# Convolution stage of a two-layer trunk: wider copies of y, statistics of the last chunk by token, another order around the norm, three tap groups on another engine

## The chip, the cores and the metric

The kernel runs on one core of a Trainium2 chip. The metric is the device time of one execution in microseconds. Three executions of the kernel before took 1098.86, 1101.70 and 1102.46 us. The core has five engines with a queue each: TensorE (PE) for matrix products, VectorE (DVE), ScalarE (ACT) and GpSimd (POOL) for elementwise work, and SyncE (SP), whose queue here issues nearly all DMAs. Each queue is worked off in order; an instruction that waits holds up all that is queued behind it.

## The reference

Two layers run over 256 latent and 256 context tokens of width 1024. The first layer's mixer is a convolution module, and the change lies in it:

```
y = h @ w1 + b1;  a, gt = split(y);  y = a * sigmoid(gt)
y = depthwise_conv(y, dw, width 31, padding 15) + dw_b
y = silu(layer_norm(y, norm_g));  return y @ w2
```

The layer norm is over the 1024 channels of a token: it takes off the mean and scales by the inverse deviation. Each sub-layer has a shift, a scale and a gate, which come from SiLU(c) @ ada_w + ada_b; a SwiGLU FFN follows, then the second layer (retention, FFN). All is float32; products with weights are made in three passes of a split into a high and a low part.

## The kernel before, in words

Channels lie on partitions, in eight chunks of 128; the 512 columns are the 256 latent and the 256 context tokens. A loop over eight steps (L633) makes the chunks one after the other. In step s TensorE makes the two halves of W1's product for chunk s (`pair_half`, 24 matmuls each, L573), and GLU gives y of chunk s: by ScalarE and GpSimd, for chunk 7 by VectorE (`glu`, L470). The 31 taps of a chunk's depthwise convolution are divided: the first 4 x GROUPS[ch] go to TensorE, the last POOL[ch] to ScalarE and GpSimd, those between to VectorE (`dwconv_dve`, L530), one instruction each over 128x512. `GROUPS` (L49) has 4 for every chunk, so a chunk has 16 taps on TensorE and 9 on VectorE, 10 for chunk 7. In step s VectorE works on chunk s-1: five taps, then the low part of the next W1 block (`w1_lo`), then `total(s-2)`, the sum of the three partial results, then the other taps.

For TensorE's taps, y goes through DRAM. `bounce_out` (L483) writes it with one DMA. `bounce_in` (L489) loads a table `dg` and then reads y back with four DMAs, shifted by 0 to 3 columns, so that each partition of `z4` holds one of 32 channels of four quarters at one of four shifts. One run of such a read is 569 numbers, 2,276 bytes. `dwconv_pe` (L500) then makes four taps with each group: four fp32 matmuls onto 32 partitions each, which the profile counts as eight. Every DMA of this part is issued by SP, in program order.

`square` and `stats` (L562, L566) sum a chunk's values and squares over its channels into four rows of a PSUM tile `pst`. After chunk 7, ScalarE copies `pst` to `srow`; TensorE turns it by token into `ptk` (L752) and spreads the mean over all partitions into `pmd` (L755); ScalarE copies that to `mb`, and GpSimd takes it off all eight chunks (L771). VectorE makes the inverse deviation in 14 small instructions (L773 to L796), TensorE spreads it (`token_row`, L776), and a loop over chunks (L815) multiplies (`z_norm`), takes the Silu on ScalarE and splits z in two parts. Then come the products with W2 in two halves of columns, n = 0 and 1, each of 96 matmuls (8 k, 4 token tiles, 3 passes).

Around this, 20 blocks of ada_w are worked in as filler. A block has four parts: `begin` (16 matmuls of sums on TensorE), `evict` (ScalarE), `cols` (TensorE, 4 short matmuls) and `finish` (ScalarE). Blocks 8 to 15 run between step 7 and z, 16 and 17 in the z loop, 18 and 19 in the first half of W2. Their rows are loaded into whatever buffer is free: two large tiles that the W1 activations leave (`fills`), the two `z4` buffers, small tiles for the blocks in `ADA_K4`, or the three buffers for weight rows (`raw`). `gate_to_rows` and `gate_bc` (L280, L293) send the gate through DRAM so that the residual after W2 can use it.

Instructions marked with `pin` keep the order in which the program gives them; the others, among them most of W2's products, are put in place by the planner that builds the queues. The order in this stage is thus mostly written out by hand.

Of the kernel before, what the change touches and what calls it, by code (L numbers as in the profile page):

```python
# [47 lines left out]
K_PAIRS = 2  # L48
GROUPS = [4, 4, 4, 4, 4, 4, 4, 4]  # L49
POOL = [6, 6, 6, 6, 6, 6, 6, 5]  # L50
# [11 lines left out]
PACC = 2  # L62
ADA_AUX = (16, 17, 18, 19)
ADA_K4 = (8, 9, 18)
T2 = 5
# [16 lines left out]
def trunk_kernel(ctx: ExitStack, tc, x_in, ctx_in, cond, small, consts, rope, dist, ada, adas, adat,  # L82
# [483 lines left out]
    def stats(ch):  # L566
        for i, src in enumerate((yc[:, ch, :], sqs.pop(ch))):
            q = 2 * (ch % 2) + i
            pin(nc.tensor.matmul(pst[32 * q:32 * q + 32, :], mean32, src, start=(ch < 2), stop=(ch >= KC - 2)))

# [138 lines left out]
    dve_taps(d, 0, cut)  # L709
    total(c)  # L710
    dve_taps(d, cut, TAPS)

    fills = [pA.tile([P, 4096], F32, tag=tag, name=f"raw_fill_{tag}") for tag in ("ah", "al")]
    pin(nc.gpsimd.memset(fills[0][:, 0:1], 0.0))
    for i in range(12, 16):
        t = fills[(i - 12) // 2][:, 2048 * (i % 2):2048 * (i % 2) + 2048]
# [3 lines left out]
    for i in (16, 17):  # L720
        t = cv.tile([P, 4, 2 * YW], F32, tag="z4", name=f"raw_ada{i}", bufs=Z4).rearrange("p q t -> p (q t)")[:, 0:2048]
        pin(nc.sync.dma_start(t, ada[ADA_PE.index(i)]))
        ada_raws[i] = halves(t)
    cols(8)
# [9 lines left out]
    evict(10)  # L734
    stats(c)
    cols(10)
    finish(10)
    begin(11)
    cbs[d] = dwconv_pe(d, zs4.pop(d))
    evict(11)  # L740
    cols(11)
    total(d)
    finish(11)
    square(d)
    stats(KC - 1)
    begin(12)
    srow = t2("srow")
    pin(nc.scalar.activation(srow, pst, AF.Copy))
    evict(12)
    ptk = aux("stats_t")  # L750
    for t in range(4):
        pin(nc.tensor.matmul(ptk[:, 2 * t:2 * t + 2], srow[:, P * t:P * t + P], sel2, start=True, stop=True))  # L752
    pmd = aux("mean_bc")
    for q in range(4):
        pin(nc.tensor.matmul(pmd[32 * q:32 * q + 32, :], sel2[:, 0:1].to_broadcast([P, 32]), srow, start=True, stop=True))  # L755
    mb = cv.tile([P, 512], F32, tag="sq", name="mb", bufs=2)
    begin(13)
    cols(12)
    pin(nc.scalar.activation(mb, pmd, AF.Copy))
    evict(13)  # L760
    finish(12)
    cols(13)
    finish(13)
    gate_to_rows(0, 0, pin)
    gates = [gate_bc(0, 0, 0, pin), gate_bc(0, 0, 1, pin)]
    ada_raws[18] = ada_load(18, pin)
    ada_raws[19] = ada_load(19, pin)
    begin(14)
    evict(14)
    for ch in range(KC):  # L770
        pin(nc.gpsimd.tensor_tensor(yc[:, ch, :], yc[:, ch, :], mb, op=ALU.subtract))  # L771
    st = cv.tile([P, 4, 2], F32, name="st")
    nc.vector.tensor_copy(st.rearrange("p t i -> p (t i)"), ptk[:, 0:8])  # L773
    md, vv = st[:, :, 0], st[:, :, 1]

# [21 lines left out]
    prs = token_row(rn, "rstd_bc")  # L797
    cols(14)
    finish(14)
    begin(15)  # L800
    evict(15)
    cols(15)
    finish(15)

# [10 lines left out]
    for ch in range(KC):  # L815
# [5 lines left out]
        if ch == W2_AT:  # L821
            split_w2(0, 1, None, pin)
        if ch in (2, 4):
            begin(15 + ch // 2)
            evict(15 + ch // 2)
        if ch in (3, 5):
            cols(15 + ch // 2)
            finish(15 + ch // 2)
# [34 lines left out]
    for n in range(2):  # L863
# [7 lines left out]
        for t, k in order:  # L871
# [3 lines left out]
            if k == KC - 1:  # L875
                residual(t, n, pw[t], gates[t // 2], last)
            if not n and t == 3 and k in (3, 5):
                begin(18 + k // 5)
                evict(18 + k // 5)
            if not n and t == 3 and k in (4, 6):  # L880
                cols(18 + k // 6)
                finish(18 + k // 6)
            if n and (t, k) == (1, KC - 1):
# [567 lines left out]
```

## Time and profile before

| what | value |
|---|---|
| profiled execution | 1103.33 us, of which 1101.2 us are the span from first to last instruction |
| median of the runs | 1101.70 us (1098.86 to 1102.46) |
| PE / DVE / ACT / POOL busy, of the span | 97% / 64% / 38% / 15% |
| mean granted TensorE clock | 0.991 of full speed |
| chain that ended last | PE 86%, DVE 6%, DMA 4%, ACT 3%, issue 1% |
| DMA | 190 MB, mean 173 GB/s |
| z from yd, 32 DMAs of 284.5 KB | median 4.9 us from issue to landing |

Times in the views count from the start of the span. In a timeline a row has its start, its duration, the engine, the line, the operation, the result and the sources, and in brackets the idle time of the engine ahead of it with what ended it. In a table of windows each engine has its busy time and its count of instructions; the last three numbers are the granted clock (1.00 is full), the mean busy share of the DMA engines and the rate in GB/s. A matmul row lasts longer than its turn, since matmuls overlap; the chain shows the turns.

### The profile page before, as it was taken

Reading aid. Unit: us, or ns where it says so; the run is one execution under the profiler, and the core shown is the slowest. Engines: PE = TensorE matmul, PEld = TensorE weight load, DVE = VectorE, ACT = ScalarE, POOL = GpSimd, SP = SyncE. Lnnn points to the kernel's source line nnn. Section 1 sums busy time; section 2 is a strip of 40 time slices with the busy share of each in tenths; the row PEclk is TensorE's granted clock in tenths of the full one; section 3 lists DMA queues with packets and bytes.
Section 4 is the critical chain, followed back from the end, with each engine's and each line's share of the span. In section 5 each row is a group of like instructions: output and inputs, shape, how many; then the busy total and the mean of one; then the engine's idle time right before and its main releaser. Section 6 shows DMA issues by size and latency. Waiting matters only on the chain.

```text
span 1101.2 us, 13492 instructions
## 1 busy us (share of the span) xinstructions
PE 1069.0 (97%) x5302; PEld 845.0 (77%) x5302; DVE 700.6 (64%) x1147; ACT 417.5 (38%) x607; POOL 161.6 (15%) x119
## 2 busy tenths in 40 slices
PE   6989998999999999999999999999999989999998
PEld 2766654789888888888888788888888868888886
DVE  3988873757999877545644796366364555555445
ACT  4474463343222122212232564234333454444442
POOL 0077853030000000000000330000000461000000
PEclk8999998999999999999999999999999999999999
DMA  9469778732566576533313342334333344455551
GB/s 372 181 179 264 223 195 348 265 115 99 191 248 249 201 296 234 186 114 116 115 59 132 135 143 106 115 134 155 113 115 115 115 152 155 172 190 191 190 182 49
DMA packets 35185, 190.29 MB, mean 173 GB/s; under 512 B 3953, under 2 KB 4401, under 8 KB 16177
## 3 DMA queue, kind: packets, MB, share of 16 engines
q1 hardware_dynamic: 34688, 187.87, 49.0%
q10 hardware_dynamic: 434, 1.55, 0.4%
q8 instruction: 42, 0.69, 0.3%
q14 instruction: 21, 0.17, 0.0%
HBM read 185.99 MB, written 3.42 MB: 172 GB/s over the span
## 4 chain that ended last, share of the span: by engine, by line
PE 86%; DVE 6%; DMA 4%; ACT 3%; issue 1%; SPq 0%; POOL 0%; ACTq 0%; DVEq 0%
PE u L202 4%; PE fa L201 4%; PE u L200 4%; PE u L201 4%; PE fa L202 4%; PE fb L201 4%; PE fb L202 4%; PE fa L200 4%; PE fb L200 4%; PE v L201 3%; PE v L202 3%; PE v L200 3%; PE dn L201 3%; PE dn L202 3%; PE dn L200 3%; PE cv L507 2%
## 5 line engine op out<-in xcount | busy, mean ns | idle before, releaser
L171 DVE TENSOR_TENSOR wl_gu<-raw_gu,wh_gu 128x1024 fp32r<-128x1024 f32 x76 | 92.2, 1223 | 82.6 <-ACT wh_gu L163 81.7
L163 ACT ACTIVATE wh_gu<-raw_gu 128x1024 fp32r<-128x1024 f32 x84 | 88.0, 1058 | 139.6 <-PE fb L201 52.6
L851 DVE SCALAR_TENSOR_TENSOR junk<-raw_adat,crow 128x1024 f32<-128x1024 f32 x80 | 97.5, 1219 | 0.9
L171 DVE TENSOR_TENSOR wl_dn<-raw_dn,wh_dn 128x1024 fp32r<-128x1024 f32 x38 | 46.5, 1224 | 45.3 <-ACT wh_dn L163 45.0
L200 PE MATMUL fa<-ah_h0f,wh_gu 128*128 128x512 f32 (+1 forms) x192 | 72.0, 376 | 1.0 <-DVE ah_h0f L324 1.0
L201 PE MATMUL fa<-al_h0f,wh_gu 128*128 128x512 f32 (+1 forms) x192 | 72.3, 376 | 0.1
L200 PE MATMUL fb<-ah_h0f,wh_gu 128*128 128x512 f32 (+1 forms) x192 | 72.1, 376 | 0.0
L202 PE MATMUL fa<-ah_h0f,wl_gu 128*128 128x512 f32 (+1 forms) x192 | 72.0, 375 | 0.0
L202 PE MATMUL fb<-ah_h0f,wl_gu 128*128 128x512 f32 (+1 forms) x192 | 72.0, 375 | 0.0
L201 PE MATMUL fb<-al_h0f,wh_gu 128*128 128x512 f32 (+1 forms) x192 | 72.0, 375 | 0.0
L163 ACT ACTIVATE wh_dn<-raw_dn 128x1024 fp32r<-128x1024 f32 x38 | 40.3, 1060 | 80.1 <-PE dn L202 35.5
L200 PE MATMUL u<-wh_gu,ah_h1f 128*128 128x512 f32 x160 | 63.5, 397 | 0.0
L171 POOL TENSOR_TENSOR wl_qk<-raw_qk,wh_qk 128x1024 fp32r<-128x1024 f32 x4 | 9.6, 2401 | 362.8 <-DVE res L355 350.3
L202 PE MATMUL u<-wh_gu,al_h1f 128*128 128x512 f32 x160 | 62.8, 393 | 0.0
L201 PE MATMUL u<-wl_gu,ah_h1f 128*128 128x512 f32 x160 | 62.2, 390 | 0.0
L523 POOL TENSOR_TENSOR pacc<-pacc,pr 128x512 f32<-128x512 f32 x39 | 58.8, 1508 | 17.8 <-ACT pr L522 15.5
L540 DVE SCALAR_TENSOR_TENSOR lacc<-y,sm,lacc 128x512 f32<-128x512 f32 x65 | 49.1, 755 | 2.1
L201 PE MATMUL v<-wl_v,ah_h 128*128 128x512 f32 x128 | 50.4, 393 | 0.0
L202 PE MATMUL v<-wh_v,al_h 128*128 128x512 f32 x128 | 50.1, 391 | 0.0
L200 PE MATMUL dn<-wh_dn,ah_hid 128*128 128x512 f32 x128 | 49.9, 390 | 0.0
L201 PE MATMUL dn<-wl_dn,ah_hid 128*128 128x512 f32 x128 | 49.8, 389 | 0.0
L202 PE MATMUL dn<-wh_dn,al_hid 128*128 128x512 f32 x128 | 49.8, 389 | 0.0
(308 smaller groups left out, 2669.5 us busy)
## 6 DMA issues: line engine op xcount, KB each, us to landing
raw_gu<-in_gu_dram SPq DMA_DIRECT2D x44, 1024.0 KB, 4.8
raw_adat<-in_adat_dram SPq DMA_DIRECT2D x28, 1024.0 KB, 4.9
raw_dn<-in_dn_dram SPq DMA_DIRECT2D x19, 1024.0 KB, 4.8
raw_ada<-in_ada_dram SPq DMA_DIRECT2D x10, 1024.0 KB, 10.8
z<-yd SPq DMA_DIRECT2D x32, 284.5 KB, 4.9
raw_qk<-in_wqk_dram SPq DMA_DIRECT2D x8, 1024.0 KB, 4.7
raw_v<-in_wv_dram SPq DMA_DIRECT2D x8, 1024.0 KB, 4.8
raw_g<-in_wg_dram SPq DMA_DIRECT2D x8, 1024.0 KB, 4.8
```

The lines of the kernel that those rows point to most:

```text
L163: also(nc.scalar.activation(hi[:, :m], raw[:, c:c + m], AF.Copy))
L171: also((eng or nc.vector).tensor_tensor(lo[:, :m], raw[:, c:c + m], hi[:, :m].bitcast(F32), op=ALU.subtract))
L200: also(nc.tensor.matmul(o, a[0], b[0], start=first, stop=False))
L201: also(nc.tensor.matmul(o, a[0], b[1], start=False, stop=False))
L202: also(nc.tensor.matmul(o, a[1], b[0], start=False, stop=last))
L507: pin(nc.tensor.matmul(cb[32 * q:32 * q + 32, :], dg[:, g, q, :], m, start=(g == 0), stop=(g == n - 1)))
L523: pin(nc.gpsimd.tensor_tensor(pacc, pacc, pr, op=ALU.add))
L540: pin(nc.vector.scalar_tensor_tensor(cacc, a, w, cacc, op0=ALU.mult, op1=ALU.add))
L851: pin(nc.vector.scalar_tensor_tensor(junk, raw[:, c, :], 1.0, crow[:, s, :], op0=ALU.mult, op1=ALU.mult, accum_out=mods[l][:, c0 + c, s:s ...
```

## The change

`GROUPS` becomes 3 for chunks 2, 3 and 4: 12 taps on TensorE and 13 on VectorE there.

y lies in DRAM as 32 rows of four quarters. It is written by four DMAs, one for each quarter, and each of the four reads has one run of 2,285 numbers (9,140 bytes) for a partition in place of four runs.

The sums of chunks 0 to 6 close ahead of chunk 7. Their copy, their turn by token and their part of the mean move ahead of `dwconv_pe(7)`. Chunk 7's values and squares are summed by token with products of one column into `ptk`, and its mean is added to `pmd` in place; VectorE adds both parts in `st`.

The order around it: blocks 12 and 13 alone lie between chunk 7 and z. Blocks 14 and 15 go into the z loop, 16 and 17 into the first half of W2, 18 and 19 into the second. The gate's rows come after z of chunk 1. Of the two large tiles only the first is filled, released on VectorE in place of GpSimd. Blocks 14 and 15 are loaded into the `z4` buffers, 16 into small tiles, and 17, 18 and 19 into the buffers for weight rows, 18 and 19 alternately with the two parts of W2's second half.

```diff
-GROUPS = [4, 4, 4, 4, 4, 4, 4, 4]
+GROUPS = [4, 4, 3, 3, 3, 4, 4, 4]
-ADA_AUX = (16, 17, 18, 19)
-ADA_K4 = (8, 9, 18)
+ADA_AUX = (14, 15, 16, 17, 18, 19)
+ADA_K4 = (8, 9, 16)
@@ bounce_out
-        yd = dr.tile([4, 32, 2 * YW], F32, name=f"yd{ch}")
-        pin(nc.sync.dma_start(yd.rearrange("q c t -> (q c) t"), y.rearrange("p s t -> p (s t)")))
+        yd = dr.tile([32, 4, 2 * YW], F32, name=f"yd{ch}")
+        for q in range(4):
+            pin(nc.sync.dma_start(yd[:, q, :], y[32 * q:32 * q + 32].rearrange("c s t -> c (s t)")))
@@ bounce_in
-        w = 2 * YW - 3
+        w = 8 * YW - 3
+        zf, yf = z4.rearrange("p q t -> p (q t)"), yd.rearrange("c q t -> c (q t)")
         for s in range(4):
-            pin(nc.sync.dma_start(z4[32 * s:32 * s + 32, :, 0:w], yd[:, :, s:s + w].rearrange("q c t -> c q t")))
+            pin(nc.sync.dma_start(zf[32 * s:32 * s + 32, 0:w], yf[:, s:s + w]))
@@ stats
-  ... stop=(ch >= KC - 2)))
+  ... stop=(ch >= KC - 3)))
@@ behind step 7
-    fills = [pA.tile([P, 4096], F32, tag=tag, name=f"raw_fill_{tag}") for tag in ("ah", "al")]
-    pin(nc.gpsimd.memset(fills[0][:, 0:1], 0.0))
-    for i in range(12, 16):
...
+    fill = pA.tile([P, 4096], F32, tag="ah", name="raw_fill")
+    pin(nc.vector.memset(fill[:, 0:1], 0.0))
     dve_taps(d, cut, TAPS)
+    for i in (12, 13):
...
     stats(c)
+    begin(11)
+    srow = t2("srow")
+    pin(nc.scalar.activation(srow, pst, AF.Copy))
     cols(10)
     finish(10)
-    begin(11)
+    evict(11)
+    ptk = aux("stats_t")
+    for t in range(4):
+        pin(nc.tensor.matmul(ptk[:, 2 * t:2 * t + 2], srow[:, P * t:P * t + P], sel2, start=True, stop=True))
+    st = cv.tile([P, 8], F32, name="st")
+    pin(nc.vector.tensor_copy(st, ptk[:, 0:8]))
+    pmd = aux("mean_bc")
+    for q in range(4):
+        pin(nc.tensor.matmul(pmd[32 * q:32 * q + 32, :], sel2[:, 0:1].to_broadcast([P, 32]), srow, start=True, stop=False))
+    cols(11)
     cbs[d] = dwconv_pe(d, zs4.pop(d))
...
     total(d)
     finish(11)
     square(d)
-    stats(KC - 1)
     begin(12)
     evict(12)
+    for i, src in enumerate((yc[:, d, :], sqs.pop(d))):
+        if i:
+            pin(nc.tensor.matmul(pmd, mean32[:, 0:1].to_broadcast([P, P]), yc[:, d, :], start=False, stop=True))
+        for t in range(4):
+            pin(nc.tensor.matmul(ptk[:, 16 + 2 * t + i:17 + 2 * t + i], src[:, P * t:P * t + P], mean32[:, 0:1],
+                                 start=True, stop=True))
+    pin(nc.vector.tensor_tensor(st, ptk[:, 16:24], st, op=ALU.add))
+    pin(nc.scalar.activation(mb, pmd, AF.Copy))
+    cols(12)
     begin(13)
+    finish(12)
     evict(13)
-    gate_to_rows(0, 0, pin)
-    gates = [gate_bc(0, 0, 0, pin), gate_bc(0, 0, 1, pin)]
-    begin(14) ... finish(15)
...
     prs = token_row(rn, "rstd_bc")
+    cols(13)
@@ z loop
+        if ch == 0:
+            finish(13)
+        if ch == 1:
+            gate_to_rows(0, 0, pin)
+            gates = [gate_bc(0, 0, 0, pin), gate_bc(0, 0, 1, pin)]
         if ch in (2, 4):
-            begin(15 + ch // 2)
+            begin(13 + ch // 2)
...
-    for i in range(2):
-        w2r[1, i] = load(w2[1, i], name=f"w2_1{i}", also=pin)
+    w2r[1, 0] = load(w2[1, 0], name="w2_10", also=pin)
+    ada_raws[18] = ada_load(18, pin)
+    w2r[1, 1] = load(w2[1, 1], name="w2_11", also=pin)
+    ada_raws[19] = ada_load(19, pin)
@@ products with W2
-            if not n and t == 3 and k in (3, 5):
-                begin(18 + k // 5)
+            if not n and t == 3 and k in (3, 6):
+                begin(16 + k // 5)
...
+            if n and t < 2 and k == 3:
+                begin(18 + t)
+                evict(18 + t)
+            if n and t < 2 and k == 5:
+                cols(18 + t)
+                finish(18 + t)
```

More of the change, by code (lines that the diff above doesn't have):

```diff
@@ L719, in trunk_kernel @@
     w2r[0, 1] = load(w2[0, 1], name="w2_01", also=pin)
[L720 to L723, printed above, removed]
     cols(8)
@@ L735, in trunk_kernel @@
     stats(c)
+    begin(11)
+    srow = t2("srow")
+    pin(nc.scalar.activation(srow, pst, AF.Copy))
     cols(10)
     finish(10)
-    begin(11)
-    cbs[d] = dwconv_pe(d, zs4.pop(d))
-    evict(11)
-    cols(11)
+    evict(11)
[8 more added lines that the diff above has]
+    cols(11)
+    cbs[d] = dwconv_pe(d, zs4.pop(d))
+    for i in (14, 15):
+        t = cv.tile([P, 4, 2 * YW], F32, tag="z4", name=f"raw_ada{i}", bufs=Z4).rearrange("p q t -> p (q t)")[:, 0:2048]
+        pin(nc.sync.dma_start(t, ada[ADA_PE.index(i)]))
+        ada_raws[i] = halves(t)
+    ada_raws[16] = ada_load(16, pin)
+    ada_raws[17] = ada_load(17, pin)
     total(d)
@@ L744, in trunk_kernel @@
     square(d)
-    stats(KC - 1)
     begin(12)
-    srow = t2("srow")
-    pin(nc.scalar.activation(srow, pst, AF.Copy))
     evict(12)
[L750 to L755, printed above, removed]
+    for i, src in enumerate((yc[:, d, :], sqs.pop(d))):
[5 more added lines that the diff above has]
+    pin(nc.vector.tensor_tensor(st, ptk[:, 16:24], st, op=ALU.add))
     mb = cv.tile([P, 512], F32, tag="sq", name="mb", bufs=2)
+    pin(nc.scalar.activation(mb, pmd, AF.Copy))
+    cols(12)
     begin(13)
-    cols(12)
-    pin(nc.scalar.activation(mb, pmd, AF.Copy))
+    finish(12)
     evict(13)
-    finish(12)
-    cols(13)
-    finish(13)
-    gate_to_rows(0, 0, pin)
-    gates = [gate_bc(0, 0, 0, pin), gate_bc(0, 0, 1, pin)]
[L766 to L769, printed above, removed]
     for ch in range(KC):
         pin(nc.gpsimd.tensor_tensor(yc[:, ch, :], yc[:, ch, :], mb, op=ALU.subtract))
-    st = cv.tile([P, 4, 2], F32, name="st")
-    nc.vector.tensor_copy(st.rearrange("p t i -> p (t i)"), ptk[:, 0:8])
-    md, vv = st[:, :, 0], st[:, :, 1]
+    md, vv = (st.rearrange("p (t i) -> p t i", i=2)[:, :, i] for i in range(2))
     def token_row(cols, name):
```

24 lines of the change are left out of this document (9 added, 15 removed).

## The prediction, made before the result was known

> **What bounds the kernel now.** I read the span and the shares of the chain first, then the chain around the changed stage, then the engine timelines of that stage, then windows of 3 us for the granted clock. The chain is TensorE for 86% of the span; the change touches the stretch from about 95 us to 236 us. There the chain reads (start, duration, what):
>
> ```profile
> span 1101.2 us, 13492 instructions
> ```
>
> ```profile
> 158.20 7.58 DMA z<-yd
> ...
> 165.92 5.37 PE cv L507 x32
> ...
> 171.31 0.70 DVE yc L630
> ...
> 174.72 0.98 PE stats_t L752 x8
> 175.71 0.99 PE mean_bc L755 x8
> ...
> 179.35 0.28 PE gr L286
> 179.62 1.00 PE ada L239 x16
> 180.62 1.09 PE rstd_bc L780 x8
> 181.71 0.34 PE ada L251 x4
> ...
> 184.68 0.59 ACT zs L819
> 185.29 0.70 DVE ah_z L324
> ...
> 186.03 0.50 PE w L200
> 186.53 0.23 PE w L201
> ```
>
> The reader should see one serial chain: the last chunk's copy back from DRAM, its TensorE taps, its statistics, the inverse deviation, the first z, and at 186.03 the first product with W2. From the end of the last sum (171.31 + 0.70 = 172.01) to that product are 14.02 us. Before and behind this chain TensorE is full, which three windows show (the first column behind the window is PE busy):
>
> ```profile
> 100.00:150.00 50.00, 50.00 (x287) 32.50 (x280) 38.09 (x44) 25.21 (x38) 40.87 (x30) 1.00 0.85 249
> ```
>
> ```profile
> 186.03:215.20 29.17, 29.16 (x170) 21.52 (x171) 21.32 (x30) 12.19 (x20) 1.29 (x2) 0.94 0.74 262
> 215.20:236.00 20.80, 20.80 (x99) 17.38 (x98) 12.02 (x30) 6.25 (x12) 1.06 (x1) 1.00 0.44 177
> ```
>
> So TensorE work taken out ahead of 154 us is time saved, work put into the W2 products behind 186 us is time lost, and between them waits decide.
>
> **Part 1, taps of chunks 2, 3 and 4 back to VectorE.** TensorE loses one group of four in each of three chunks; VectorE gains 12 taps.
>
> ```profile
> 143.95 3.62 PE L507 MATMUL cv<-z,dg 128*32 128x512 f32 x32
> ```
>
> ```profile
> 95.29 0.76 DVE L538 TENSOR_SCALAR lacc<-y,sm 128x512 f32<-128x512 f32 x1 [2.13 <-POOL y L480]
> ...
> 109.52 0.75 DVE L538 TENSOR_SCALAR lacc<-y,sm 128x512 f32<-128x512 f32 x1 [1.88 <-POOL y L480]
> ...
> 119.19 3.12 DVE L540 SCALAR_TENSOR_TENSOR lacc<-y,sm,lacc 128x512 f32<-128x512 f32 x4
> 124.34 0.75 DVE L538 TENSOR_SCALAR lacc<-y,sm 128x512 f32<-128x512 f32 x1 [2.03 <-POOL y L480]
> ...
> 128.17 3.65 DVE L171 TENSOR_TENSOR wl_w1b<-raw_w1b,wh_w1b 128x1024 fp32r<-128x1024 f32 x2
> ...
> 139.73 0.75 DVE L538 TENSOR_SCALAR lacc<-y,sm 128x512 f32<-128x512 f32 x1 [3.48 <-POOL y L480]
> ...
> 147.64 0.69 DVE L630 TENSOR_TENSOR yc<-yc,cv 128x512 f32<-128x512 f32 x1 [3.40 <-PE cv L507]
> ```
>
> TensorE: 32 products of a chunk last 3.62 us, so a group is 0.9 us and three are 2.7 us. VectorE: four taps are 3.12 us, so 9.4 us are added, against idle time of 2.13, 1.88, 2.03 and 3.48 = 9.5 us ahead of the taps of chunks 3 to 6. Since TensorE makes each next y 0.9 us sooner, I carry the lateness along: chunk 3's taps start 3.12 - 2.13 = 1.0 us behind their y; chunk 4's 1.0 + 3.12 - (1.88 - 0.9) = 3.1; chunk 5's 3.1 + 3.12 - (2.03 - 0.9) = 5.1; chunk 6's 5.1 - (3.48 - 0.9) = 2.5, and the 3.40 us for which VectorE waits at 147.64 takes that up with 0.9 left. What queues behind late taps is the split of the next W1 block, for which TensorE waits: the one at 128.17 now ends at 131.82, would end at 131.8 - 1.8 + 5.1 = 135.1, and its second half is wanted half-way through a product block that starts about 135, so it is just in time. The gain lies between 2.7 us (TensorE's own) and a loss of 0.5 (VectorE keeps the 2.5 us of lateness and more); I take 2.5, since each wait is just covered.
>
> **Part 2, the copies of y.** One DMA out becomes four, the four in read runs of 9 KB in place of 2.3 KB. All are on SP, with the table load and the fills queued behind. The trace has no such DMA. Bounds: three more issues of about 0.4 us put the landing at most 1.1 us later than 158.20 + 7.58 = 165.78, that is 166.9, if the long runs are no faster; if they move like the 1 MB weight rows (4.8 us from issue to landing, quoted below) they land near 163. Neither matters, because Part 3 keeps TensorE busy until 166.7. I take nothing; if that cover were gone, the faster end would be worth the 1.7 us that TensorE waits from 164.2 to 165.92.
>
> **Part 3, statistics by token.** Sums of chunks 0 to 6 now close early; their transposed sums (0.98), the mean's broadcast (0.99) and the columns of block 11 (0.34 in the chain's row, some 0.5 with their start) run ahead of chunk 7's taps.
>
> ```profile
> 163.14 1.07 PE L239 MATMUL ada<-raw_ada,csil 128*32 128x256 f32 x16
> ```
>
> ```profile
> 164.00:167.00 3.00, 1.29 (x12) 0.46 (x12) 0.25 (x1) 0.39 (x1) 0.00 (x0) 0.86 0.88 349
> 167.00:170.00 3.00, 3.00 (x20) 0.97 (x16) 0.00 (x0) 0.00 (x0) 0.00 (x0) 0.57 1.00 421
> ...
> 185.00:188.00 3.00, 1.97 (x6) 1.59 (x7) 2.59 (x5) 1.48 (x3) 2.32 (x2) 0.78 0.97 265
> 188.00:191.00 3.00, 3.00 (x22) 1.35 (x21) 2.97 (x5) 0.26 (x2) 0.00 (x0) 0.66 0.99 367
> ```
>
> The seventh number behind the window's length and busy columns is the granted clock: it falls to about half behind each of the two waits. That is why chunk 7's taps take 5.37 us instead of 3.62, so one such stretch costs 1.75 us. With work in the wait, the taps run 164.2 + 0.98 + 0.99 + 0.5 = 166.7 to 170.3 at full clock, against 171.29: 1.0 us gained. The copy of the statistics row on ScalarE (0.60 us, the first row below) lies beside block 11's 1.07 us on TensorE.
>
> **Part 4, the norm's chain first.** Behind the last sum now come, on TensorE, what is left of block 12 (0.3), four products of yc (0.98 for four), the mean, and four products of the squares (0.98), in this chain with one column each.
>
> ```profile
> 91.91 0.86 PE mean L580 x2
> ```
>
> ```profile
> 173.90 0.60 ACT L748 ACTIVATE srow<-stats 128x512 f32<-128x512 f32 x1 [1.14 <-PE stats L569]
> ```
>
> ```profile
> 177.44 9.88 POOL L771 TENSOR_TENSOR yc<-yc,mb 128x512 f32<-128x512 f32 x8 [14.87 <-DVE stats_t L794]
> ```
>
> ```profile
> 175.75 0.17 DVE L773 COPY st<-stats_t 128x8 f32<-128x8 f32 x1 [3.74 <-PE stats_t L752]
> ...
> 178.23 0.16 DVE L796 SCALAR_TENSOR_TENSOR rn<-stats_t,rn 128x4 f32<-128x4 f32 x1
> 181.82 1.28 DVE L810 TENSOR_TENSOR zt<-yc,rstd_bc 128x512 f32<-128x512 f32 x2 [3.43 <-PE rstd_bc L780]
> ```
>
> VectorE's part is 175.75 to 178.39 = 2.64. Today the broadcast then starts at 180.62, 2.2 us late, because the gate's transpose and block 14 stand ahead of it on TensorE; and the first Silu at 184.68, 2.2 us after its input at 182.5, because block 15's steps stand ahead of it on ScalarE. With these moved behind: 0.3 + 0.98 + 0.86 + 0.98 + 2.64 + 1.09 + 0.64 + 0.59 + 0.70, and some 0.5 for nine hand-overs, is 9.3 us against 14.02: 4.7 gained. Products with one column are not in the trace; at half of 0.98 it would be 1.0 better, at twice, 2.0 worse; I take 0.98, as the two-column row is nearest. GpSimd's subtraction of the mean starts at +2.9 and gives a chunk each 9.88 / 8 = 1.24 us, ahead of z.
>
> **Part 5, what is pushed back.** Blocks 14 and 15 and the gate's transpose now run inside the W2 products, where TensorE has nothing free: 2 x (1.00 + 0.34) + 0.28 = 3.0 us lost. On SP, the second half of W2's right block now needs a buffer and its turn behind block 17, near the end of the first 96 products.
>
> ```profile
> raw_w<-in_w_dram SPq DMA_DIRECT2D x4, 1024.0 KB, 10.8
> ```
>
> ```profile
> raw_gu<-in_gu_dram SPq DMA_DIRECT2D x44, 1024.0 KB, 4.8
> ```
>
> ```profile
> L171 DVE TENSOR_TENSOR wl_gu<-raw_gu,wh_gu 128x1024 fp32r<-128x1024 f32 x76 | 92.2, 1223 | 82.6 <-ACT wh_gu L163 81.7
> L163 ACT ACTIVATE wh_gu<-raw_gu 128x1024 fp32r<-128x1024 f32 x84 | 88.0, 1058 | 139.6 <-PE fb L201 52.6
> ```
>
> Counted from the end of those products: block 17's sums are over at about -3.1 (twelve products of 0.23 and 0.34 for its columns are still to come). Landing 4.8 us later, ScalarE 1.06 and VectorE 1.22 make the first half ready at +4.0. It is wanted at +3.8 (twelve products and block 18's 1.00), and VectorE has the residuals of the first half to do beside it. I take 0.6 lost; bounds 0 and the price of the second rival. Queued behind that load are block 19, the condition rows and the first FFN weights; these have over 5 us in hand.
>
> **The sum.** -2.5 - 1.0 - 4.7 = -8.2 at the first W2 product, +3.0 + 0.6 behind it: -4.6 us. The profiled execution took 1103.33 us (1101.2 span, 2.1 around it), so 1098.7 for it; the runs shown have a median of 1101.7, 1.6 lower, so 1097.1. Everything behind 236 us keeps its work.
>
> **The rivals.**
> (a) VectorE becomes the bound in the convolution. For: 9.4 us into 9.5 us of idle time. Against: the 3.40 us wait that ends on TensorE. The 2.5 us go, leaving -2.1: 1099.6.
> (b) Slower: the W2 half whose load now stands behind block 17. For: four loads of W2 near here took a median of 10.8 us, not 4.8. Against: the DMA engines were busy for 0.74 of that stretch (the window from 186.03), and the rows of blocks 14 to 18 have landed by then. At 10.8 the half is ready at +10.0, 6.2 us late, and such an idle stretch brings a half-clock stretch of 1.75: 8.0 in place of 0.6, so +2.8: 1104.5. It decides from a landing of about 8 us on.
> (c) The W2 products start at full clock. The row at 185 shows half clock behind a wait of 1.8 us, and the changed chain still has waits of 1.2 and 1.7 us there, with 1.6 us of work between them; so the sum has the stretch unchanged. If the gate does not close, 1.75 is saved: -6.3, 1095.4. The Trainium skill ("TensorE: Matmul & The Clock Gate", part 1) has the clock halved after a whole idle window of about 3.4 us; by that rule this would be the case. The trace does not agree: both half-clock stretches here follow idle times of less than 2 us.
> (d) The copies do not do what they say: runs of 9 KB, two to each of 16 DMA engines, go slower. For: nothing in the trace has this shape. If their 7.58 us become half as much again, they land at 166.9 + 3.8, TensorE waits 4.0 us and pays 1.75 for the clock: +5.7, in all +1.1, 1102.8. Against: 8 KB rows are the fastest loads here.
>
> **How the numbers follow.** Forecast 0.50 (own range 1095.7 to 1098.7), (a) 0.17, (b) 0.10, (c) 0.15, (d) 0.08. A measurement of this kernel can tell about 0.3%, 3.3 us, from no change: the limits are 1098.4 and 1105.0. Faster: 0.85 of the forecast and all of (c), 0.57. Slower: less than half of (b) and a third of (d), 0.07. Same: 0.36. Range 1093.0 to 1102.5: it takes in (a), (c) with TensorE's full 2.7 and the cheaper products, and the forecast; (b) and most of (d) stay out.
>
> **What would show it.** Part 1: y of chunk 7 about 2.5 us sooner, VectorE's idle ahead of the taps of chunks 3 to 5 gone. Part 2 and 3: no TensorE wait for z ahead of chunk 7's taps, and these last 3.6 us at clock 1.00. Part 4: about 9.3 us from the last sum to the first W2 product, no block's step between the inverse deviation, its broadcast and the first Silu. Part 5: W2's 192 products and their blocks 3 us longer; a TensorE wait, if any, in the middle of the first token tile of the right half. I am wrong if the first W2 product starts less than 6 us sooner, or if the span falls by less than half of what that start gains.

## The result and the profile after

The changed kernel is slower: 1110.76 us median of four executions (1110.39 to 1112.57) against 1100.28 of the kernel before on the same chip (1098.04 to 1102.46), ratio 1.0094, 95% interval 1.0076 to 1.0111. The forecast was 1097.1. The profiled execution took 1110.39 us, 7.06 more than the profiled one of before, where 4.6 less had been forecast. One execution each of the kernel before (1187.72 us) and of two versions further down (1187.77 and 5734.71 us) stands far outside the others and is left out of all medians and ratios.

The four landmarks below come from the timelines of both kernels; the last two rows add up to where the time went.

| landmark, us | before | after | difference |
|---|---|---|---|
| last y (chunk 7) starts on VectorE | 153.54 | 151.55 | -1.99 |
| last sum done (end of `yc` of chunk 7) | 172.00 | 168.82 | -3.18 |
| first W2 product | 186.03 | 181.78 | -4.25 |
| first transpose of the next norm | 234.91 | 241.58 | +6.67 |
| span | 1101.2 | 1108.6 | +7.4 |

So the first W2 product does start sooner, but by 4.25 us and not by 8.2; then 10.92 us are lost between it and the first transpose (59.80 against 48.88), and behind that only 0.7.

The chain of waits of the changed kernel (start, duration, what), cut to the two places in question:

```profile
171.92 0.99 DVE mq L791
172.93 1.20 DVE va L792
174.15 1.19 DVE rn L795
177.37 2.06 PE rstd_bc L784 x8
...
181.78 0.79 PE w L200
...
234.09 1.06 ACT wh_gu L163
235.48 2.13 DVE modA L270
```

Two things here are in none of the steps that the prediction followed. Three of VectorE's small statistics instructions, of four columns each, take 0.99, 1.20 and 1.19 us (0.16 to 0.17 before). And at the end of W2 the chain leaves TensorE: it goes through the split of the first FFN weight on ScalarE (`wh_gu`) and through `modA`, the scales of the next norm.

The first place, VectorE and GpSimd side by side in the timeline of the changed kernel:

```profile
171.60 9.82 POOL L777 TENSOR_TENSOR yc<-yc,mb 128x512 f32<-128x512 f32 x8 [11.08 <-ACT mb L771]
171.72 0.17 DVE L769 TENSOR_TENSOR st<-stats_t,st 128x8 f32<-128x8 f32 x1 [2.90 <-PE stats_t L767]
171.92 0.98 DVE L791 TENSOR_TENSOR mq<-st 128x4 f32<-128x4 f32 x1
172.93 1.19 DVE L792 SCALAR_TENSOR_TENSOR va<-st,mq 128x4 f32<-128x4 f32 x1
174.15 1.19 DVE L795 TENSOR_SCALAR rn<-va 128x4 int32<-128x4 int32 x1
175.26 0.15 DVE L796 TENSOR_SCALAR stats_t<-va 128x4 f32<-128x4 f32 x1
```

GpSimd's eight subtractions last 1.23 us each, so the first three end at about 172.83, 174.06 and 175.28. `mq` ends at 172.90, `va` at 174.12, `rn` at 175.34: each slow instruction ends as a subtraction ends. Two others in the same stretch are not slowed: the sum `st`, one of whose inputs is in PSUM (0.17), and the last row, whose result goes to PSUM (0.15).

What TensorE does meanwhile and behind it, in windows of 3 us of the changed kernel (length, busy of the five engines with PEld second, then granted clock, DMA share, GB/s):

```profile
173.00:176.00 3.00, 0.13 (x4) 0.00 (x0) 2.86 (x6) 0.38 (x1) 3.00 (x3) 0.73 0.99 408
176.00:179.00 3.00, 1.63 (x7) 1.66 (x8) 1.02 (x7) 0.00 (x0) 3.00 (x4) 0.50 1.05 425
...
182.00:185.00 3.00, 3.00 (x8) 2.26 (x9) 2.93 (x5) 0.05 (x1) 0.00 (x0) 0.56 0.02 5
```

TensorE is idle for 4.24 us ahead of `rstd_bc`, which then runs at half clock (2.05 us; 1.16 before), and so do the first W2 products, as some did before.

The second place, in the timelines. Before:

```profile
225.62 0.50 PE L251 MATMUL ada<-cst,adasb 128*128 128x2 f32 x4
226.16 0.41 ACT L258 ACTIVATE mods<-ada,sm 128x2 f32<-128x2 f32 x2 [4.75 <-PE ada L251]
226.60 0.18 DVE L270 SCALAR_TENSOR_TENSOR modA<-mods,sm 128x16 f32<-128x16 f32 x1 [0.49 <-ACT mods L258]
```

After:

```profile
234.34 0.50 PE L251 MATMUL ada<-cst,adasb 128*128 128x2 f32 x4
234.09 1.06 ACT L163 ACTIVATE wh_gu<-raw_gu 128x1024 fp32r<-128x1024 f32 x1 [4.09 <-PE w L202]
235.05 0.40 ACT L258 ACTIVATE mods<-ada,sm 128x2 f32<-128x2 f32 x2
235.22 2.36 POOL L171 TENSOR_TENSOR wl_gu<-raw_gu,wh_gu 128x1024 fp32r<-128x1024 f32 x1 [53.79 <-ACT wh_gu L163]
235.48 2.13 DVE L270 SCALAR_TENSOR_TENSOR modA<-mods,sm 128x16 f32<-128x16 f32 x1 [8.92 <-ACT mods L258]
241.58 1.48 PE L342 MATMUL tr<-cst,xn 128*128 128x128 f32 x4 [5.71 <-DVE xn L312]
```

Block 19's columns stand 8.7 us later in TensorE's queue, behind some 32 products of token tiles 2 and 3 (before, just ahead of tile 2). Its last step, `mods`, stands on ScalarE behind `wh_gu`, which the changed order has ahead of it; that adds little, since the columns end at 234.84 and `mods` starts at 235.05. The norm's squares (`xn`) are queued behind `mods`. `modA` starts 8.9 us later and takes 2.13 in place of 0.18, again up to the end of a GpSimd instruction (235.22 + 2.36 = 237.58; 235.48 + 2.13 = 237.61). This costs at most 0.1 us, because ScalarE's squares, for which VectorE waits next, end at 237.52; the first `xn` on VectorE counts for more, 1.55 us beside GpSimd's next split instead of 0.75. TensorE runs out of products and waits 5.71 us. The windows there, first of before and then of after:

```profile
236.00:239.00 3.00, 2.43 (x13) 1.68 (x11) 1.22 (x3) 2.90 (x6) 3.00 (x2) 1.00 0.00 0
```

```profile
236.00:239.00 3.00, 0.00 (x0) 0.00 (x0) 2.93 (x10) 2.47 (x5) 2.04 (x2) 1.00 0.00 0
239.00:242.00 3.00, 0.42 (x1) 0.18 (x1) 3.00 (x9) 0.00 (x0) 1.88 (x1) 0.54 0.11 14
```

With the 3.0 us counted for blocks 14 and 15, the 5.7 of this wait make 8.7 of the 10.92; the other 2.2 lie where TensorE is busy (54.1 us against 48.9, at a mean clock of 0.96 and 0.97), and I don't split them further. The half clock behind the wait falls into the next stretch.

### The profile page after: what moved, and what is told of

Its sections match the earlier page's. It is cut to its first block, busy times and chain, and to the rows that moved or that the text cites. A ratio compares the mean times of both kernels' runs of the same rounds, so it can differ in the third digit from the quotient of the medians.

```text
span 1108.6 us, 13524 instructions
## 1 busy us (share of the span) xinstructions
PE 1070.6 (97%) x5292; PEld 847.7 (76%) x5292; DVE 715.5 (65%) x1161; ACT 417.1 (38%) x607; POOL 161.3 (15%) x118
## 3 DMA queue, kind: packets, MB, share of 16 engines
q10 hardware_dynamic: 434, 1.55, 0.4%
## 4 chain that ended last, share of the span: by engine, by line
PE 88%; DVE 5%; ACT 3%; DMA 2%; issue 1%; POOL 1%; SPq 0%; ACTq 0%; DVEq 0%; POOLq 0%
PE u L202 4%; PE u L200 4%; PE fa L201 4%; PE u L201 4%; PE fa L202 4%; PE fa L200 4%; PE fb L202 4%; PE fb L201 4%; PE fb L200 4%; PE v L201 3%; PE v L202 3%; PE v L200 3%; PE dn L201 3%; PE dn L200 3%; PE dn L202 3%; PE g L202 2%
## 5 line engine op out<-in xcount | busy, mean ns | idle before, releaser
L542 DVE SCALAR_TENSOR_TENSOR lacc<-y,sm,lacc 128x512 f32<-128x512 f32 x77 | 58.2, 755 | 2.5
```

What stands on the lines that cost most here:

```text
L542: pin(nc.vector.scalar_tensor_tensor(cacc, a, w, cacc, op0=ALU.mult, op1=ALU.add))
```

## The experiments

The theory from these rows: two new waits make the loss, VectorE's small instructions beside GpSimd (some 3 us and the clock behind them) and block 19's late end (some 7 us); the rest of the change does about what the sum said. Its rivals: the copies, the taps, or the loads cost the time.

The ratios below are to the kernel before, measured beside each version. The changed kernel was not measured again beside them, so a difference from its 1110.76 us is one between sessions, and the kernel before moved by up to 1.7 us between them. Of the versions made from the changed kernel, only the written order and the two that combine mends have intervals clear of its 1.0076 to 1.0111; for the others the timelines carry the argument, one profiled execution each.

**All of W2's second half in the written order.** The planner may no longer put products of tiles 0 and 1 ahead of the blocks.

```
-            last = pin if n and t > 1 else (lambda i: None)
+            last = pin if n else (lambda i: None)
```

> The changed kernel with one edit: all products of the right half of W2 keep the program's order, not those of the last two token tiles alone, so that block 19's columns stand on TensorE ahead of the third token tile and its last step on ScalarE stands ahead of the first FFN weight. Theory A (the time went into the end of W2: block 19 is finished at 235 us, behind a weight split on ScalarE that waits for W2's buffers, so the norm of the FFN starts late, TensorE waits 6.7 us and then runs at half clock): that wait goes, the FFN's first products come about 8 us sooner, and the kernel is 7 to 9 us faster than the changed one, about 1.001 to 1.003 of the kernel before. Rival B (the late load of the second half of W2's right block is the cost): TensorE now waits in the middle of the first token tile for it, and the time does not fall by more than 2 us.

Measured: 1105.11 us, ratio to before 1.0022 (1.0010 to 1.0034), 5.65 us by the medians under the changed kernel's 1110.76, 7.9 by the ratios. In the timeline `mods` of block 19 stands ahead of the weight's split, `modA` takes 0.17 us again, and TensorE goes into the transposes without a wait; from the first W2 product to the first transpose are 54.79 us instead of 59.80.

```profile
232.81 0.41 ACT L258 ACTIVATE mods<-ada,sm 128x2 f32<-128x2 f32 x2 [1.47 <-PE ada L251]
233.26 0.17 DVE L270 SCALAR_TENSOR_TENSOR modA<-mods,sm 128x16 f32<-128x16 f32 x1 [4.71 <-ACT mods L258]
241.14 1.06 ACT L163 ACTIVATE wh_gu<-raw_gu 128x1024 fp32r<-128x1024 f32 x1 [4.21 <-PE w L202]
```

So the largest part of the loss is the place of block 19, not the amount of work. The profiled execution was the slowest of ten (1109.56; the fastest was 1102.27). It lost time far ahead, at chunk 1's taps: a wait for the copy of 2.84 us (1.77 in the changed kernel), and 6.60 us for products that take 3.64 at full clock.

```profile
84.22 6.60 PE L509 MATMUL cv<-z,dg 128*32 128x512 f32 x32 [2.84 <-DMA z<-yd]
```

**Two of the small statistics tiles in PSUM.**

```
-    mq = cv.tile([P, 4], F32, name="mq")
-    va = cv.tile([P, 4], F32, name="va")
+    mq, va = ptk[:, 24:28], ptk[:, 28:32]
```

> The changed kernel with one edit: the squared mean and the variance (8 columns) lie in PSUM, not in SBUF, so the three small VectorE instructions that had SBUF on every side have PSUM on one. Theory C (these three took 0.98, 1.19 and 1.19 us in place of 0.16 each because they wait for GpSimd's subtractions of the mean, which now start ahead of them): each takes about 0.16 again, the broadcast starts 2.9 us sooner and at full or nearly full clock, the first W2 product comes 3 to 5 us sooner, and the kernel is 3 to 5 us faster than the changed one, 1.005 to 1.007 of the kernel before. Rival D (they wait for something else, such as the sums' arrival): the three stay at about 1 us each.

Measured: 1108.60 us, 1.0063 (1.0047 to 1.0079). From the last sum to the first W2 product 10.92 us instead of 12.96. `va` and `rn`, which now have an operand in PSUM, fall to 0.17 and 0.16; `mq`, whose result is now in PSUM but whose two inputs are still in SBUF, does not:

```profile
172.14 0.99 DVE L790 TENSOR_TENSOR stats_t<-st 128x4 f32<-128x4 f32 x1
173.16 0.17 DVE L791 SCALAR_TENSOR_TENSOR stats_t<-st,stats_t 128x4 f32<-128x4 f32 x1
```

**GpSimd held back.** This tells GpSimd from the loads that land in the same stretch.

```
+    pin(nc.gpsimd.tensor_copy(mq, rn))
+    for ch in range(KC):
+        pin(nc.gpsimd.tensor_tensor(yc[:, ch, :], yc[:, ch, :], mb, op=ALU.subtract))
     prs = token_row(rn, "rstd_bc")
```

(the same loop is taken out further up)

> The changed kernel with GpSimd's eight subtractions of the mean held back until VectorE's chain to rstd is done (GpSimd first copies rn, then subtracts). Theory (GpSimd's operations slow VectorE's small operations whose operands all lie in SBUF): mq, va and the first rn fall from 0.98, 1.19 and 1.19 us to about 0.17 each, the last rn comes 2.9 us sooner after the last sum; the first zt then waits for the first subtraction (1.23 us after the last rn) or for rstd_bc (up to 2.05): last sum to first W2 product about 10 us in place of 12.96, and the time 1.5 to 3 us under the changed kernel's. Rival (the four loads of blocks 14 to 17, which land in the same stretch, slow VectorE's access to SBUF): the three operations stay near 1 us each, and the distance to the first W2 product grows by about 0.5 to 1.2 us.

Measured: the three instructions, again with all operands in SBUF, take 0.16, 0.16 and 0.17 us, and it is 9.62 us from the last sum to the first W2 product:

```profile
174.37 0.16 DVE L789 TENSOR_TENSOR mq<-st 128x4 f32<-128x4 f32 x1
174.57 0.16 DVE L790 SCALAR_TENSOR_TENSOR va<-st,mq 128x4 f32<-128x4 f32 x1
174.77 0.17 DVE L793 TENSOR_SCALAR rn<-va 128x4 int32<-128x4 int32 x1
...
176.88 0.19 POOL L799 COPY mq<-rn 128x4 f32<-128x4 f32 x1 [13.89 <-DVE rn L798]
177.03 9.92 POOL L801 TENSOR_TENSOR yc<-yc,mb 128x512 f32<-128x512 f32 x8
```

GpSimd's running subtractions are the cause; the loads still land in this stretch (434 GB/s from 174 to 175 us). The time, 1109.35 us (1.0066, 1.0053 to 1.0079), is 1.4 under the changed kernel's, just short of what was expected; in the profiled execution chunk 1's taps lost time again (5.34 us behind a wait of 2.37), so that its last sum came 2.46 later than the changed kernel's.

**Four groups again.** `GROUPS` back to 4 for chunks 2, 3 and 4, the rest as changed.

> The changed kernel with four tap groups on TensorE for all chunks again. If the three groups on VectorE brought what the traces show (y of chunk 7 2.0 us sooner), chunk 7's y comes at about 153.5 us again and the kernel is about 2 us slower than the changed one, 1.011 of the kernel before. If VectorE's added 9.4 us cost as much elsewhere, no difference: 1.009.

Measured: 1115.42 us, 1.0117 (1.0100 to 1.0134): 4.7 us slower than the changed kernel by the medians, 2.5 by the ratios, whose intervals overlap. The last y comes 2.1 us later, and chunk 7's taps fall to the half clock behind a wait of 0.94 us in spite of part 3:

```profile
167.54 5.08 PE L509 MATMUL cv<-z,dg 128*32 128x512 f32 x32 [0.94 <-DMA z<-yd]
```

**The old copies.** `bounce_out` and `bounce_in` as before, the rest as changed.

> The changed kernel with y copied as before: one DMA out, four DMAs in with runs of 2.3 KB. The prediction's step (the copies are hidden, since TensorE is busy until chunk 7's taps can start): no difference from the changed kernel, 1.009 of the kernel before, with no TensorE wait ahead of chunk 7's taps. Rival: the copies out in four cost SP and the chain 0.7 us and more, then it is 1 us faster or more; or the runs of 9 KB help, then TensorE waits for z and it is 1 to 3 us slower.

Measured: 1109.86 us, 1.0071 (1.0057 to 1.0084). The last y is written at 150.09 instead of 151.55, and the last sum comes 1.45 us sooner; none of that reaches the end in the profiled execution, whose span is the same 1108.6.

**Reads without a shift.**

```
-            pin(nc.sync.dma_start(zf[32 * s:32 * s + 32, 0:w], yf[:, s:s + w]))
+            pin(nc.sync.dma_start(zf[32 * s:32 * s + 32, 0:w], yf[:, 0:w]))
```

> The changed kernel with all four reads of a set starting at the same element: the three copies of y shifted by one, two and three tokens are not made, so TensorE's taps use unshifted data; everything else is computed as before. Theory (a start that is off by 4, 8 or 12 bytes slows the reads, whatever the length of a run): the four reads of a set land in about 3.7 us (500 / 710 of the shifted packets' time) in place of 4.9, and TensorE's wait for chunk 1's z, 1.8 us in the changed kernel, shrinks by about 1 us. Rival (the rate is set by something else, such as the 32 partitions that each read writes): landing stays at 4.9 us and the wait at 1.8.

Measured: 1110.12 us in one execution. The reads land no sooner, 5.3 us with the same start against 4.9 with shifted ones (the row without a shift; the last number is the median):

```profile
z<-yd SPq DMA_DIRECT2D x32, 285.6 KB, 5.3
```

My theory that the shifted start costs the time falls. What sets the rate of these reads stays open.

**Part 1 alone**, on the kernel before.

```
-GROUPS = [4, 4, 4, 4, 4, 4, 4, 4]
+GROUPS = [4, 4, 3, 3, 3, 4, 4, 4]
```

> The kernel before with one edit, the groups of taps of chunks 2, 3 and 4 from four to three. Theory (VectorE's taps are late there, part 1 of the change is worth its own saving): chunk 7's y is written about 2 us sooner (151.5), everything to the first W2 product moves with it, the rest of the kernel stays: time 1099.6, 2 us under before. Rival 1: what follows is tied to loads or to TensorE, and the 2 us are lost ahead of W2: no change, 1101.6. Rival 2: the shift puts block 19 or the planner's order at the end of W2 in another place: slower than before by 1 us or more.

Measured: 1097.52 us against 1102.02, ratio 0.9959 (0.9946 to 0.9973). One line of the change beats both kernels, the one before by 4.5 us, twice what I expected. In the timeline the last y starts at 150.63 (153.54 before), and TensorE waits only 0.52 us for the copy, so that chunk 7's taps stay at full clock; the last sum is done at 166.20, 5.8 us sooner than before. Of these, 2.9 are the y's, 1.2 the copy's (from the start of y to the taps 11.18 us instead of 12.38) and 1.7 the clock's (3.64 instead of 5.34). Why the copy came sooner behind y no run shows:

```profile
161.81 3.64 PE L507 MATMUL cv<-z,dg 128*32 128x512 f32 x32 [0.52 <-DMA z<-yd]
```

**Parts 1 and 2 alone.** The same, with the new copies.

> The kernel before with three groups of taps for chunks 2, 3 and 4 and with the copies of y in runs of 9 KB (parts 1 and 2 of the change without the rest). Theory (the copies cost what the run with old copies gave back): chunk 7's y is written 0.9 to 1.5 us later than with the groups alone (151.5 to 152.1), the time is 1 to 1.5 us above it, 1098.8 to 1099.3, with single executions some 4 us longer where chunk 1's taps fall to the half clock behind a wait of over 2.2 us. Rival (the copies cost nothing, as the prediction had it): same time as with the groups alone, 1097.8.

Measured: 1099.53 us, 0.9987 (0.9974 to 0.9999); without the new copies it was 0.9959 (0.9946 to 0.9973), and the intervals just miss each other. The medians, from two sessions, differ by 2.0 us, the ratios by 0.28%, 3.1 us. In the profiled execution SP is busy 1.72 us with issuing one set of writes, and the last sum comes 1.15 us later than with the groups alone (167.35):

```profile
151.93 1.72 SPq L487 DMA_DIRECT2D yd<-y  x4
```

With one DMA for the set, in the run with the groups alone, it is 0.34 us. Of the 1.15 us, 0.53 are there at the start of chunk 1's taps (82.74 against 82.21), and some 0.6 come at chunk 7's, where TensorE waits 1.15 us for the copy instead of 0.52. This profiled execution, at 1097.56 one of the fastest of twelve, made up most of that by its end (span 1095.7 against 1095.4); where the slower ones lost time was not profiled.

**Three mends together:** written order, two tiles in PSUM, old copies, in the changed kernel.

> The changed kernel with three edits at once: all products of W2's second half kept in the written order, the two small statistics tiles mq and va in PSUM, and the copies of y as they were before. Theory (three separate prices, each seen alone so far): they add. Last sum at 167.4 us as with the old copies alone, 10.9 us from there to the first W2 product (178.3), 54.8 from there to the first transpose (233.1), then 98.7 and 766.7 to the end: span 1098.6, time about 1100.4, the time of the kernel before. Rival 1: the loss at the end of W2 returns once its start is sooner, because the late load of W2's second half then binds by more (its issue is tied to block 17): first product to first transpose 57 or more, time 1103 or more. Rival 2: the clock decides and not the waits: half-clock stretches appear elsewhere, and the time lies anywhere from 1100 to 1108 with a spread over 4 us between executions.

Measured: 1100.75 us, 0.9988 (0.9979 to 0.9997). The last sum comes at 167.71, the first W2 product at 177.71 (10.00 us), the first transpose at 232.39 (54.68 us), span 1098.0. So the three prices about add up to the loss (5.65, 2.16 and 0.90 alone, 10.0 together, by the medians): without them, the change is about where the kernel before was. But it is also 3 us slower than part 1 alone.

**Three more mends:** `mq` with an input in PSUM, block 14 behind the rstd transposes, block 18 back in W2's first half (15, 16 and 17 move by a step or two with it).

> The three edits of the run with old copies, PSUM tiles and written order, and three more: the token sums are added a second time into PSUM, so that mq too has an operand there; block 14's sums go behind the rstd transposes, into TensorE's idle time ahead of the first W2 product; block 18 goes back into W2's first half, with blocks 16 and 17 one or two steps sooner, so that W2's second right half and block 19's weights are issued sooner. Theory: last sum 167.4, 10.1 us to the first W2 product (177.5), 51.5 to the first transpose (48.9 as before, 1.5 for block 15, 1.0 for the gate's transposes), span 1094.5, time about 1096.3, some 5 us under the kernel before. Rival 1 (the late W2 half binds whatever the blocks do): TensorE waits for it at the start of the second half, first product to first transpose 54 or more, time 1099 or more. Rival 2 (block 14 ahead of the first product delays it): last sum to first product 11 or more.

Measured: 1101.48 us, 0.9992 (0.9980 to 1.0004); the theory's 1096.3 was missed, and rival 2's sign is there, 12.21 us from the last sum to the first product. All of VectorE's small instructions took 0.16 to 0.17 us, and yet `rstd_bc` ran at half clock again (2.05 us): the clock fell at 171 us, though no wait of TensorE is listed in the 30 us ahead. At the end of W2's first half TensorE waits 1.28 us in one window, and another stretch at half clock begins, of 6.8 us:

```profile
209.00:212.00 3.00, 1.72 (x21) 1.05 (x21) 3.00 (x5) 2.84 (x7) 0.00 (x0) 0.99 0.28 46
212.00:215.00 3.00, 3.00 (x9) 2.57 (x10) 1.53 (x2) 0.41 (x2) 0.00 (x0) 0.50 0.97 336
```

This was the profiled execution, at 1104.18 one of the slower ones (the fastest took 1097.38); how often that stretch occurs is not known.

**Part 1 and the order that part 4 was after, without the rest.** In the run of part 1 alone TensorE starts `rstd_bc` 2.16 us after its input is there, and ScalarE's first `zs` stands behind the last steps of blocks 14 and 15:

```profile
172.43 0.16 DVE L796 SCALAR_TENSOR_TENSOR rn<-stats_t,rn 128x4 f32<-128x4 f32 x1
...
173.74 1.07 PE L239 MATMUL ada<-raw_fill_al,csil 128*32 128x256 f32 x16
174.75 1.16 PE L780 MATMUL rstd_bc<-cst,rn 128*128 128x128 f32 x8
...
178.75 1.30 ACT L819 ACTIVATE zs<-zt,sm 128x512 f32<-128x512 f32 x2
...
180.22 0.50 PE L200 MATMUL w<-wh_w,ah_z 128*128 128x512 f32 x1 [1.81 <-DVE ah_z L324]
```

```
     finish(13)
-    gate_to_rows(0, 0, pin)
...
-    begin(14)
-    evict(14)
...
     prs = token_row(rn, "rstd_bc")
-    cols(14)
...
+    begin(14)
     begin(15)
...
+        if ch == 0:
+            evict(14)
+            evict(15)
+            cols(14)
...
+        if ch == 1:
+            gate_to_rows(0, 0, pin)
...
```

> The kernel before with three groups of taps for chunks 2, 3 and 4, and one more edit: the gate's transpose goes behind the second chunk of z, and blocks 14 and 15 are summed behind the rstd transposes, their rows and columns behind the first chunk of z (in the run with the groups alone TensorE stood at 174.75 to start rstd_bc though rn was ready at 172.59, and ScalarE started the first zs at 178.75, behind the mods of blocks 14 and 15, though zt was there at 176.7). Theory (the order of TensorE's and ScalarE's queues is what held the chain): rstd_bc starts by 173.2, the first zs by 175.2, the first W2 product at 176.5 in place of 180.22, the gate's transpose costs 0.3 us later: time 3.4 us under the run with the groups alone, about 1094.4. Rival 1 (blocks 14 and 15 then stand in TensorE's queue ahead of the first product or hold PSUM that it needs): first product not before 178.5, time 1096 or more. Rival 2: W2's end is upset again (block 19 or the FFN's weight split ahead of it), time above 1098.

Measured: 1091.47 us against 1100.63, ratio 0.9915 (0.9899 to 0.9931): the fastest version, 9.2 us under the kernel before.

```profile
172.50 1.14 PE L776 MATMUL rstd_bc<-cst,rn 128*128 128x128 f32 x8
173.56 1.93 PE L239 MATMUL ada<-raw_fill_al,csil 128*32 128x256 f32 x32
176.53 0.48 PE L200 MATMUL w<-wh_w,ah_z 128*128 128x512 f32 x1
```

The first product starts at 176.53, where the theory had 176.5, with blocks 14 and 15 done in what was TensorE's idle time. The gain is 5.9 us of span over part 1 alone (1089.5 against 1095.4) and not 3.4. A part that I had not priced is the clock. The windows of part 1 alone, and then of this run:

```profile
179.00:182.00 3.00, 1.77 (x6) 1.48 (x7) 2.43 (x4) 1.48 (x3) 2.52 (x3) 0.88 0.10 40
182.00:185.00 3.00, 3.00 (x20) 1.09 (x19) 2.93 (x6) 0.27 (x1) 0.00 (x0) 0.55 0.94 326
```

```profile
179.00:182.00 3.00, 3.00 (x16) 2.38 (x14) 2.15 (x5) 0.84 (x2) 2.31 (x2) 1.00 1.04 421
182.00:185.00 3.00, 3.00 (x25) 1.82 (x24) 1.06 (x2) 1.49 (x3) 0.00 (x0) 1.00 0.55 225
```

With the idle time filled, the clock is not halved at W2's start: 1.7 us by the sum of (1 - clock) over the two windows. That the filled idle time is the reason is likely, not shown.

## Why the prediction was wrong

**The direction was wrong** for two reasons. In the profiled pair, the way to the first W2 product was 4.0 us longer than forecast (4.25 gained, not 8.2), and what lies behind it 8.1 (11.7 lost, not 3.6). The step that decided is in part 5: the three sentences on what waits behind the late load. They followed the load of W2's half and called block 19 safe with "over 5 us in hand". The 5 us were for its data; its columns on TensorE and its last step on ScalarE were placed by the planner, behind some 32 products and behind the FFN weight's split, the norm of the FFN waited for them, and TensorE for the norm (5.71 us). No rival named that. The run with the written order took back 5 us of the way from first product to first transpose.

**Part 4** was mis-sized in one term: VectorE's 2.64 us measured 5.50 (171.72 to 177.22). I had written that "GpSimd's subtraction of the mean starts at +2.9" and had weighed it against z alone, not against VectorE's chain, beside which it now runs. It was known from the rows of before that GpSimd started at 177.44, when VectorE was already past `mq`, `va` and the first `rn` (175.94 to 176.51); what changed is who comes first. Held back, the chain measured 9.62 us, near my 9.3 though it then also waited for the first subtraction; as changed 12.96. Of the 3.7 us more than forecast, 2.9 are this chain's; the other 1.0 is the half clock, which I had left unchanged: `rstd_bc` at 2.05 in place of 1.09. It stayed with two tiles in PSUM (2.04) and was gone from `rstd_bc` with GpSimd held back (1.13); that VectorE's delay brought it about is not shown.

**Part 1** was right in sign, and too small on its own: predicted -2.5, measured -4.5 alone on the kernel before (5.8 in the profiled pair, of which the 2.9 of y are what the text had counted). The last y came 2.0 us sooner in the changed kernel, and VectorE's idle time ahead of the taps is gone, as the text said. Rival (a) fell: VectorE did not become the bound; at chunk 5's sum (145.63) it still waits 2.02 us for TensorE (3.16 with the groups alone).

**Part 3** did what it said (no wait ahead of chunk 7's taps, 3.64 us at clock 1.00), and with part 1 the last sum came 3.18 us sooner for 3.5 predicted. But it was priced on the wrong base. I took its gain from the wait of 1.7 us and the half clock of the kernel before. With part 1 in place that wait is 0.52 us and the clock is full already, so what remains of part 3 is its work ahead of the taps: the last sum at 167.71 with parts 1 and 3 (three mends, old copies) against 166.20 with part 1 alone. Up to the last sum it costs 1.5 us, by these two profiles; no run has part 3 by itself. The two terms were not independent, and their sum came out right by luck, while one was too small and the other had the wrong sign.

**Part 2** was costed at nothing "because Part 3 keeps TensorE busy". The cover holds for chunk 7; it was not looked for at the other chunks. Counted from the start of SP's write of chunk 1's y, its taps begin 12.0 to 12.9 us later in the seven profiles with the new copies (12.12 in the changed kernel) and 10.9 to 11.3 in the six with the old (11.08 before). In two of the seven, none of the six, the half clock followed (behind waits of 2.37 and 2.84 us). As a pair of medians the copies cost 2.0 us. Rival (d) did not happen: the reads are no slower. What costs is the part's own bound, three more issues (1.70 us on SP instead of 0.34, where 1.1 more had been estimated), which was weighed at chunk 7 alone, where the cover did hold.

**Part 5's** 3.0 us are borne out in part. With the three mends it is 54.7 us from first product to first transpose, against 48.9. Of the 5.8 more, 0.78 is a wait of TensorE and some 0.7 the clock (2.4 us lost to it against 1.7, by windows), which leaves 4.3 where 3.0 were counted; what makes the difference was not looked for.

**Rival (b)** gave the right sign for another reason. The load was issued when the text said, at 208.34 behind block 17, and ScalarE did wait for it:

```profile
213.14 2.01 ACT L163 ACTIVATE wh_w<-raw_w 128x1024 fp32r<-128x1024 f32 x2 [5.97 <-DMA raw_w<-in_w_dram]
```

TensorE did not: other products of the second half were put ahead. With the written order its one wait in the W2 products is 0.78 us ahead of block 17's columns, and what ended it was ScalarE's step for that block, not this load.

**Rival (c)** did not happen in the changed kernel (clock 0.56 in the window from 182), but it did in the fastest version, where TensorE has no idle time there at all. In the run with part 1 alone the clock fell to 0.55 behind a wait of 1.81 us with work ahead of it; the Trainium skill's rule ("TensorE: Matmul & The Clock Gate", part 1), which asks for a whole idle window of about 3.4 us, is not borne out there.

The text's own test, first product at least 6 us sooner and half of that in the span, failed in both halves: 4.25 sooner, and the span longer.

## What to carry to other kernels

Price each edit on the kernel that the other edits leave: two edits that remove the same wait don't add, and the second may be left with its cost alone. When a step is moved later, follow every part of it to its last instruction in each queue, planner's queue included, and ask what the consumer of that last part does; having its data in time is not enough. When a chain of small instructions is shortened on one engine, look at what the neighbouring engine now runs beside it.

## What the runs showed of the hardware

Small VectorE instructions with all their operands in SBUF waited for the GpSimd instruction that was running: 0.16 us alone, 0.98 to 1.19 beside subtractions of 1.23 each, 2.13 for `modA` beside a split of 2.36, each ending within 0.1 us of GpSimd's. With one input in PSUM they took 0.16 to 0.17, and with one input in SBUF and the result in PSUM 0.15; with two inputs in SBUF the result's place did not help (`mq`, 0.99). Not all were hit: the one-column steps of the next norm's inverse deviation were not slowed by the split that started at 238.54.

Longer runs did not make the copy of y faster: 4.9 us to landing with runs of 9,140 bytes, 4.9 with runs of 2,276, and a common start of the four reads didn't either (5.3).

The half clock came in stretches of 3.4, 6.8, 10.2 or 13.7 us between 60 and 255 us of the thirteen traces, so it can cost well over the wait ahead of it. The length of that wait does not decide alone. At chunk 7's taps with four groups again, 0.94 us brought it; at chunk 1's, behind 2.03 (two tiles in PSUM) and 2.06 (the fastest version), the clock stayed full for the next 10 us. What decides stays open. Executions of one version differ by several us (1102.27 to 1109.56 with the written order); whether these stretches make the difference is not shown, since one execution of each was profiled.
